# A gate table stored in reading order, with the expert gathers spread over the table's building

## The chip, the cores and the metric

The kernel runs on one NeuronCore of a Trainium2 chip. The metric is the device time of one execution in microseconds (us), the median of several runs. Engines are named as the profile names them: PE (TensorE matmuls; PEld are its weight loads), DVE (VectorE), ACT (ScalarE), POOL (GpSimd, which also issues the gathers) and SP (SyncE, which issues most loads).

## The reference, cut to what matters

One decoder block over 256 tokens of width 2048 in fp32. The first sub-layer (sparse attention and a pooling mixer) is not touched. The second is the PEER retrieval: 8 heads pick 16 of 16384 single-neuron experts for each token.

```python
q = jnp.einsum('bsd,de->bse', h, w_peer_q).reshape(B, S, PEER_HEADS, 2, PEER_QDIM // 2)
sub = jnp.einsum('bshpd,hpnd->bshpn', q, peer_keys, ...)
s_top, i_top = lax.top_k(sub, PEER_TOPK)
cand = s_top[..., 0, :, None] + s_top[..., 1, None, :]
...
best, pos = lax.top_k(cand, PEER_TOPK)
experts = jnp.take_along_axis(cand_idx, pos, axis=-1)
gates = jax.nn.softmax(best, axis=-1)
...
a = jax.nn.gelu(jnp.einsum('cd,ced->ce', hc, peer_u[ec]), approximate=False)
out = jnp.einsum('ce,ced->cd', a * gc, peer_v[ec])
```

## The kernel before, in words

The kernel computes 224 of the 256 tokens densely: all 16384 experts' activations, multiplied by a gate table that is zero where an expert was not picked. The other 32 tokens (AS) are done sparsely: their experts' rows are gathered from memory and reduced on DVE. Both share the last two thirds of the time, which is a loop of 512 steps of the same size on PE. A step takes half of an expert block's table: 8 weight blocks of 128x128, each with a product with 448 columns (L934: the rounded weights `wH` with both halves of the activations) and one with 224 (L935: the remainder `wL`). Steps 0 to 255 are the up stage (table `in_u`), 256 to 383 the first down half and 384 to 511 the second (table `in_v`).

The program's order is written out by hand, engine by engine. In step k, `ahead(k)` issues a table load on SP (into one of 4 `raw` buffers) and splits the half of step k+2: a cast on ACT (`wH`, L125) and a subtraction on DVE (`wL`, L126). Then come the products, and then `spend(rate)`, which adds the rate to a credit and takes pieces of DVE work off a list of tasks until the credit is used up. A piece names its DVE time in us (0.69 for one operation of the gate building, 2.37 for a sparse reduction); a piece that names none (`yield None`) ends the step's turn. Each engine works through its own queue in order, so a piece that waits holds up all that stands behind it.

The list is, in this order: `routing(0)` (the experts of the first 128 tokens), the gate table of tokens 32 to 127, `routing(1)`, the gate table of the rest, `tokens_h`, two loads of `in_ada` left over from the first sub-layer, then 32 `sparse_up` and 32 `sparse_down`. A `sparse_up(n)` reduces the gathered rows `r` (L814, "r<-r,hs"; two buffers) and lets POOL issue the gather for n+2 (L809). `gates_build(x)` makes the gates of 8 tokens: four DVE operations on fp16 (L750, L757), 16 small matmuls (L771), and two copies on ACT (L781) into a staging tile `hs`, of which POOL writes every second one's 1 MB to `gdram` (L783). The staging tile has one buffer: its next ACT copy waits until the write has landed.

Near the end of the up stage and through the first down half, `gate_table(b)` reads 8 expert blocks' gates on SP (L906, `gb`, one buffer, so it waits for both multiplications with the last one), `gate_load` reads 4 blocks of activations `ab` from `adram` (L902), `gate_mul` multiplies them on DVE (L918), and POOL writes them back to `adram` (L923) for the second half, except for 9 of 32 groups (`kept`), which stay in the space of `hHL`. `gate_split` (L928, L929) makes the two halves that the down products take.

Of the kernel before, what the change touches and what calls it, by code (L numbers as in the profile page):

```python
# [9 lines left out]
F32 = mybir.dt.float32  # L10
F32R = mybir.dt.float32r
# [8 lines left out]
P = 128  # L20
T = 256
D = 2048
ND = 16
# [4 lines left out]
SH1, SC1, GT1, SH2, SC2, GT2 = (16 * i for i in range(6))  # L28
AS = 32
N = T - AS  # L30
# [1 line left out]
KGROUPS = ((0, 4), (4, 10), (10, 16))  # L32
NGU = 43
RAW = 4
R_K, R_Y, R_GA, R_WO, R_PQ = 0.6, 0.75, 0.7, 0.6, 0.3
TB = 8
R_UP, R_D1, R_D2 = 0.97, 0.3, 0.75
KEPT = 9
GATE_SCALE = 2.0 ** 15


# [1 line left out]
def kernel(  # L43
# [23 lines left out]
    nc = tc.nc  # L67
# [8 lines left out]
    cb = const.tile([P, D], F32, name="cb")  # L76
# [69 lines left out]
    def add_bias(i, n):  # L146
        dve.tensor_tensor(mod[:, i:i + n], modr[:, i:i + n], bada[:, i:i + n], ALU.add)
# [29 lines left out]
    bg = []  # L177
# [544 lines left out]

    def routing(t):
        for h in range(8):
            if t:
                yield from top_list(t, h)
            yield from top_cand(t, h)
        yield from decode(t, 0)
        yield from decode(t, 1)
        yield from gates_of(t)  # L730

    gdram = dram.tile([P, N // 16, P, 16], F32, name="gdram")
    adram = dram.tile([P, P, N], F32, name="adram")
    made = {}

# [38 lines left out]

    def gates_out(x):
        if x % 2 == 0:
            made["stage"] = px.tile([P, D], F32, name="hs")
        stage = made["stage"].rearrange("p (i t) -> p i t", t=16)
        for y in range(2):
            t0 = 8 * (x % 2) + 4 * y  # L780
            act.mul(stage[:, :, t0:t0 + 4], made["g", y].rearrange("p (t i) -> p i t", i=P), 1.0 / GATE_SCALE)  # L781
        if x % 2 == 1:
            nc.gpsimd.dma_start(out=gdram[:, (x - AS // TB) // 2].rearrange("p i t -> p (i t)"), in_=made["stage"])  # L783
            made["gates"] = x

    def tokens_h(q):
# [48 lines left out]
            fetch(n + 2, vrows)  # L835
        yield 2.36

    def ada_later(i):
        raw = load(ada_in[i])
        yield None  # L840
        yield None
        ada_sum(raw, i)
        yield 2.37

    def tasks_up():
        yield from routing(0)
        for x in range(AS // TB, P // TB):
            yield from gates_build(x)
        yield from routing(1)
        for x in range(P // TB, T // TB + 1):  # L850
            yield from gates_build(x)
        for q in range(4):
            yield from tokens_h(q)
        fetch(0, urows)
        fetch(1, urows)
        yield None
        for n in range(AS):
            if bg:
                yield from ada_later(bg.pop(0))
            elif "gt2" not in made:  # L860
                add_bias(GT2, 16)
                made["gt2"] = True
            yield from sparse_up(n)
        for n in range(AS):
            yield from sparse_down(n)

    work = tasks_up()
    credit[0] = 0.0

    def spend(budget):  # L870
        credit[0] = min(credit[0] + budget, 4.0)
        while credit[0] > 0.0:
            cost = next(work, "end")
            if cost is None or cost == "end":
                return cost
            credit[0] -= cost

    raws = {}

# [11 lines left out]
    def half(k):  # L891
        return split(raws[k // 2][:, 1024 * (k % 2):1024 * (k % 2) + 1024])

    def kept(h):
        return h % 3 == 0 and 0 < h <= 3 * KEPT

    def gate_load(n):
        h = n % (P // 4)
# [4 lines left out]

    def gate_table(b):
        made["gb", b] = px.tile([P, N // 16, 8, 16], F32, name="gb")
        nc.sync.dma_start(out=made["gb", b], in_=gdram[:, :, 8 * b:8 * b + 8])  # L906

    def gate_mul(h):
        if kept(h):
            if "keep" not in made:  # L910
                made["keep"] = main.tile([P, ND, 2, T], F32R, name="hHL").rearrange("p a b t -> p (a b t)")
            o = 4 * N * (h // 3 - 1)
            dst = made["keep"][:, o:o + 4 * N].bitcast(F32).rearrange("p (i n) -> p i n", n=N)
            made["ab", P // 4 + h] = dst
        else:
            dst = made["ab", h]
        i = 4 * (h % 2)
        dve.tensor_tensor(dst.rearrange("p i (g t) -> p i g t", t=16),  # L918
                          made["ab", h].rearrange("p i (g t) -> p i g t", t=16),
                          made["gb", h // 2][:, :, i:i + 4].rearrange("p g i t -> p i g t"), ALU.mult)  # L920
        made["ab", h] = dst
        if not kept(h):
            nc.gpsimd.dma_start(out=adram[:, 4 * h:4 * h + 4], in_=dst)  # L923
# [8 lines left out]
    def mm2(ps, w, off, xHL, start, stop):  # L932
        wH, wL = w[0][:, off:off + P], w[1][:, off:off + P]
        pe.matmul(ps[:, :2 * N].rearrange("p (a n) -> p a n", a=2), wH, xHL, start=start, stop=False)  # L934
        pe.matmul(ps[:, :N], wL, xHL[:, 0], start=False, stop=stop)  # L935

    engines = {mybir.EngineType.PE, mybir.EngineType.DVE, mybir.EngineType.Activation, mybir.EngineType.Pool,
               mybir.EngineType.SP}
# [30 lines left out]
    for k in range(2 * P):  # L969
        e, f = k // 2, k % 2  # L970
        ahead(k)
        if f == 0:
            ps = accp.tile([P, 512], F32, name="acc")
        w = ws.pop(k)
        for d in range(8):
            mm2(ps, w, d * P, hHL[:, 8 * f + d, :, AS:], f == 0 and d == 0, f == 1 and d == 7)
        if f == 1:
            pend.append(lambda e=e, ps=ps: up_add(e, ps))
        spend(R_UP)
        if k == 2 * P - 24:  # L980
            assert made["gates"] == T // TB - 1
            gate_table(0)
            for h in range(3):
                gate_load(h)
        if k in (2 * P - 8, 2 * P - 7):
            gate_mul(k - 2 * P + 8)
        if k == 2 * P - 6:
            gate_table(1)
        if k == 2 * P - 5:
            gate_split(0)  # L990
        if k == 2 * P - 4:
            gate_load(3)
# [22 lines left out]
        nc.sync.dma_start(out=out[:, 0:8, :], in_=xT[:, 0:8, :])  # L1015

    for hf in range(2):
        assert hf == 0 or made["gt2"]
        po = [accp.tile([P, 512], F32, name="acc") if q < 6 else gps.tile([P, 512], F32, name="gp") for q in range(8)]

        def products(e, w, j):
            mm2(po[j], w, P * j, made["act", 32 * hf + e // 4][:, e % 4], e == 0, e == P - 1)

        for e in range(P):
            k = 2 * P + P * hf + e
            h = e // 4
            if e < P - 1:
                ahead(k)
            if e < P - 2:
                w = ws.pop(k)  # L1030
# [12 lines left out]
            if hf == 0 and e % 8 == 5 and b + 2 < P // 8:  # L1043
                gate_table(b + 2)
            if e % 4 == 1 and n + 1 < 2 * (P // 4):
                gate_split(n + 1)
            if e % 4 == 2 and n + 4 < 2 * (P // 4):
                gate_load(n + 4)
            done = spend(R_D2 if hf else R_D1)
            if hf and done == "end" and "sum" not in made:  # L1050
                made["sum"] = True
                pend.append(lambda: sparse_sum(po))
                pend.append(lambda: pend.append(lambda: sparse_out(po)))
# [80 lines left out]
```

## Time and profile before

| What | us |
|---|---|
| median of 3 runs (lowest, highest) | 2155.93 (2154.45, 2156.39) |
| the profiled execution | 2165.35 |
| its span, first to last instruction | 2163.6 |
| PE busy | 2080.1 (96%) |
| DVE busy | 1704.4 (79%) |
| ACT busy | 1039.6 (48%) |
| POOL busy | 142.5 (7%) |

The profiled execution is 9.4 us longer than the median of the runs. PE is busy nearly everywhere, so time is found where it stands idle or where its weight blocks come more slowly. The up stage begins at 793.6 us of the span, the first down half at about 1486, the second at about 1825.

### The profile page before, as it was taken

Reading aid. Unit: us, or ns where it says so; the run is one execution under the profiler, and the core shown is the slowest. Engines: PE = TensorE matmul, PEld = TensorE weight load, DVE = VectorE, ACT = ScalarE, POOL = GpSimd, SP = SyncE. Lnnn points to the kernel's source line nnn. Section 1 sums busy time; section 2 is a strip of 40 time slices with the busy share of each in tenths; the row PEclk is TensorE's granted clock in tenths of the full one; section 3 lists DMA queues with packets and bytes.
Section 4 is the critical chain, followed back from the end, with each engine's and each line's share of the span. In section 5 each row is a group of like instructions: output and inputs, shape, how many; then the busy total and the mean of one; then the engine's idle time right before and its main releaser. Section 6 shows DMA issues by size and latency. Waiting matters only on the chain.

```text
span 2163.6 us, 35340 instructions
## 1 busy us (share of the span) xinstructions
PE 2080.1 (96%) x14192; PEld 1965.9 (91%) x14192; DVE 1704.4 (79%) x2424; ACT 1039.6 (48%) x1405; POOL 142.5 (7%) x120
## 2 busy tenths in 40 slices
PE   6999999999898999999999999989999999999998
PEld 4998997899898999999999999888999998999998
DVE  7888888767877778778887775877777678888855
ACT  4543342463334445555555555444544455544544
POOL 0000000000000000000000000221111012222100
PEclk8999999999899999999999999998999999999999
DMA  9887886768875656676666777999999999999964
GB/s 348 326 314 294 303 307 247 278 242 304 311 291 200 219 212 228 235 262 249 231 231 248 255 279 269 363 399 342 371 361 373 370 374 346 374 375 375 365 221 143
DMA packets 142933, 640.29 MB, mean 296 GB/s; under 512 B 11449, under 2 KB 42193, under 8 KB 94257
## 3 DMA queue, kind: packets, MB, share of 16 engines
q1 hardware_dynamic: 124690, 530.82, 67.5%
q0 software_dynamic: 13472, 92.55, 11.4%
q10 hardware_dynamic: 4608, 14.68, 1.7%
q8 instruction: 111, 1.82, 0.3%
q14 instruction: 52, 0.43, 0.1%
HBM read 595.95 MB, written 42.02 MB: 295 GB/s over the span
## 4 chain that ended last, share of the span: by engine, by line
PE 47%; issue 24%; DMA 13%; DVE 10%; ACT 3%; POOL 1%; SPq 0%; DVEq 0%; ACTq 0%; POOLq 0%
PE acc L934 16%; PE acc L935 8%; DMA raw<-in_ada_dram 6%; PE acc L137 5%; DMA raw<-in_v_dram 5%; PE acc L135 5%; PE acc L136 5%; PE gp L934 4%; DVE raw L140 4%; DVE wL L126 3%; PE gp L935 2%; ACT wH L125 2%; DMA raw<-in_u_dram 1%; PE acc L510 1%; DMA r<-in_urow_dram,idxS 0%
## 5 line engine op out<-in xcount | busy, mean ns | idle before, releaser
L125 ACT CAST wH<-raw 128x1024 fp32r<-128x1024 f32 (+2 forms) x738 | 751.1, 1022 | 926.3 <-PE acc L934 278.5
L126 DVE TENSOR_TENSOR wL<-raw,wH 128x1024 fp32r<-128x1024 f32 (+2 forms) x738 | 871.3, 1188 | 329.1 <-ACT wH L125 326.4
L934 PE MATMUL acc<-hHL,wH 128*128 128x448 f32 x2048 | 655.7, 377 | 0.5 <-ACT r L601 0.5
L935 PE MATMUL acc<-hHL,wL 128*128 128x224 f32 x2048 | 546.8, 267 | 9.3 <-DVE wL L126 9.2
L934 PE MATMUL acc<-aHL,wH 128*128 128x448 f32 x1536 | 503.6, 378 | 7.6 <-DVE ast L961 5.0
L935 PE MATMUL acc<-aHL,wL 128*128 128x224 f32 x1536 | 409.6, 267 | 6.5 <-DVE wL L126 6.2
L934 PEld LDWEIGHTS acc<-hHL,wH 128*128 128x128 f32 x2048 | 386.3, 189 | 29.2 <-ACT r L601 0.7
L935 PEld LDWEIGHTS acc<-hHL,wL 128*128 128x128 f32 x2048 | 393.3, 192 | 12.2 <-DVE wL L126 12.1
L135 PE MATMUL acc<-hHL,wH 128*128 128x256 f32 x1200 | 345.9, 289 | 19.2 <-ACT wH L125 17.9
L137 PE MATMUL acc<-hHL,wL 128*128 128x256 f32 x1200 | 342.0, 287 | 8.7 <-DVE wL L126 8.6
L136 PE MATMUL acc<-hHL,wH 128*128 128x256 f32 x1200 | 342.1, 286 | 0.1
L934 PEld LDWEIGHTS acc<-aHL,wH 128*128 128x128 f32 x1536 | 290.8, 189 | 29.8 <-DVE ast L961 5.3
L935 PEld LDWEIGHTS acc<-aHL,wL 128*128 128x128 f32 x1536 | 296.2, 193 | 12.2 <-DVE wL L126 12.1
L135 PEld LDWEIGHTS acc<-hHL,wH 128*128 128x128 f32 x1200 | 232.4, 194 | 23.9 <-ACT wH L125 21.4
L140 DVE CUSTOM_DVE_ANT_0 raw<-raw,cb 128x2048 f32<-128x2048 f32 x96 | 219.7, 2288 | 43.4 <-DMA raw<-in_ada_dram 37.6
L137 PEld LDWEIGHTS acc<-hHL,wL 128*128 128x128 f32 x1200 | 231.5, 194 | 11.8 <-DVE wL L126 11.5
L136 PEld LDWEIGHTS acc<-hHL,wH 128*128 128x128 f32 x1200 | 232.5, 194 | 0.8 <-DVE hHL L574 0.3
L934 PE MATMUL gp<-aHL,wH 128*128 128x448 f32 x512 | 177.1, 377 | 0.4 <-DVE xT L998 0.4
L935 PE MATMUL gp<-aHL,wL 128*128 128x224 f32 x512 | 135.4, 264 | 0.0
L934 PEld LDWEIGHTS gp<-aHL,wH 128*128 128x128 f32 x512 | 96.4, 188 | 8.0 <-DVE xT L998 1.0
L935 PEld LDWEIGHTS gp<-aHL,wL 128*128 128x128 f32 x512 | 98.2, 192 | 0.0
L814 DVE CUSTOM_DVE_ANT_0 r<-r,hs 128x2048 f32<-128x2048 f32 x32 | 73.2, 2287 | 15.1 <-DMA r<-in_urow_dram,idxS 15.1
(250 smaller groups left out, 2070.5 us busy)
## 6 DMA issues: line engine op xcount, KB each, us to landing
raw<-in_u_dram SPq DMA_DIRECT2D x128, 1024.0 KB, 5.1
raw<-in_v_dram SPq DMA_DIRECT2D x128, 1024.0 KB, 9.5
raw<-in_ada_dram SPq DMA_DIRECT2D x96, 1024.0 KB, 5.7
raw<-in_wgrp_dram SPq DMA_DIRECT2D x43, 768.0 KB, 6.0
ab<-adram SPq DMA_DIRECT2D x55, 448.0 KB, 8.8
raw<-in_ybr_dram SPq DMA_DIRECT2D x16, 1024.0 KB, 6.6
raw<-in_wga_dram SPq DMA_DIRECT2D x16, 1024.0 KB, 4.8
raw<-in_wout_dram SPq DMA_DIRECT2D x16, 1024.0 KB, 5.0
```

Source lines behind the costliest of these rows:

```text
L125: act.copy(wH[:, :n], src)
L126: dve.tensor_tensor(wL[:, :n], src, wH[:, :n], ALU.subtract)
L135: pe.matmul(ps, wH, xH, start=start, stop=False, **kw)
L136: pe.matmul(ps, wH, xL, start=False, stop=False, **kw)
L137: pe.matmul(ps, wL, xH, start=False, stop=stop, **kw)
L140: dve.tensor_tensor_reduce(raw, raw, cb, scale=1.0, scalar=0.0, op0=ALU.mult, op1=ALU.add, accum_out=modr[:, i:i + 1])
L510: pe.matmul(ps, ybr[0][:, o:o + P], pooled[k], start=k == 0, stop=k == 7)
L814: dve.tensor_tensor_reduce(rows, rows, made["h"], scale=1.0, scalar=0.0, op0=ALU.mult, op1=ALU.add, accum_out=aS[:, n:n + 1])
L934: pe.matmul(ps[:, :2 * N].rearrange("p (a n) -> p a n", a=2), wH, xHL, start=start, stop=False)
L935: pe.matmul(ps[:, :N], wL, xHL[:, 0], start=False, stop=stop)
```

## The change

The gate table lies in `gdram` in the order in which `gate_table` reads it: a read takes 7168 contiguous bytes per partition instead of 14 pieces of 512 bytes, and a write now makes 16 pieces of 512 bytes per partition instead of one of 8192. The staging tile is `cb` instead of `hs`; `hs` holds the sparse tokens' activations from early on. The task list becomes two streams, `gates` and `sparse`. `tokens_h` and the first two gathers come before the gate building. `spend` takes a sparse piece ahead of a gate piece whenever the sparse work so far, times 3.2, lies at least 70 us under the gate work so far. The up stage's rate is 1.0 while the gate stream lives and 0.5 after it (before: 0.97); the first down half's is 0.2 (before: 0.3). The two late loads of `in_ada` move into the projection ahead of the up stage (rate 0.45 instead of 0.3). 13 groups stay on the chip instead of 9, and the first gate table is read 14 steps ahead of the end of the up stage instead of 24.

```diff
-R_K, R_Y, R_GA, R_WO, R_PQ = 0.6, 0.75, 0.7, 0.6, 0.3
+R_K, R_Y, R_GA, R_WO, R_PQ = 0.6, 0.75, 0.7, 0.6, 0.45
-R_UP, R_D1, R_D2 = 0.97, 0.3, 0.75
-KEPT = 9
+R_UP, R_D1, R_D2 = 1.0, 0.2, 0.75
+R_SU, G_LEAD = 3.2, 70.0
+KEPT = 13
...
-    gdram = dram.tile([P, N // 16, P, 16], F32, name="gdram")
+    gdram = dram.tile([P, P // 8, N // 16, 8, 16], F32, name="gdram")
...
         if x % 2 == 0:
-            made["stage"] = px.tile([P, D], F32, name="hs")
+            made["stage"] = const.tile([P, D], F32, name="cb")
...
-            nc.gpsimd.dma_start(out=gdram[:, (x - AS // TB) // 2].rearrange("p i t -> p (i t)"), in_=made["stage"])
+            nc.gpsimd.dma_start(out=gdram[:, :, (x - AS // TB) // 2],
+                                in_=made["stage"].rearrange("p (b i t) -> p b i t", i=8, t=16))
...
+    def tasks_first():
+        yield from routing(0)
+        for h in range(8):
+            yield from top_list(1, h)
         for q in range(4):
             yield from tokens_h(q)
         fetch(0, urows)
         fetch(1, urows)
+        yield from tasks_gates()
...
     def spend(budget):
         credit[0] = min(credit[0] + budget, 4.0)
+        held = set()
         while credit[0] > 0.0:
-            cost = next(work, "end")
-            if cost is None or cost == "end":
-                return cost
-            credit[0] -= cost
+            ready = [n for n in streams if n not in held]
+            if "gat" not in made and "sparse" in ready:
+                ready.remove("sparse")
+            if "gates" in streams and "sparse" in ready and spent["sparse"] * R_SU > spent["gates"] - G_LEAD:
+                ready.remove("sparse")
+            if "sparse" in ready and "gates" in ready:
+                ready.remove("gates")
+            if not ready:
+                return
+            n = ready[0]
+            cost = next(streams[n], "end")
+            if cost == "end":
+                del streams[n]
+            elif cost is None:
+                held.add(n)
+            else:
+                credit[0] -= cost
+                spent[n] += cost
...
     def kept(h):
-        return h % 3 == 0 and 0 < h <= 3 * KEPT
+        return h % 2 == 1 and 3 <= h < 3 + 2 * KEPT
...
-        nc.sync.dma_start(out=made["gb", b], in_=gdram[:, :, 8 * b:8 * b + 8])
+        nc.sync.dma_start(out=made["gb", b], in_=gdram[:, b])
...
-        spend(R_UP)
-        if k == 2 * P - 24:
+        spend(R_UP if "gates" in streams else 0.5)
+        if k == 2 * P - 14:
```

What POOL issues during the gate building, before: the 14 writes of the gate table (`gdram<-hs`), and only then the gathers of the sparse tokens (`r<-in_urow_dram`).

```order
L783 DMA gdram<-hs 128x2048 x14
L809 DMA r_14327<-in_urow_dram,idxS 128x2048 x18
L923 DMA adram<-ab 128x896
```

The same place in the changed kernel: the writes, now of 2048 pieces each (`gdram<-cb`), and the gathers alternate.

```order
L809 DMA r_10409<-in_urow_dram,idxS 128x2048 x3
L782 DMA gdram<-cb 2048x1x128 x2
L809 DMA r_10409<-in_urow_dram,idxS 128x2048
L782 DMA gdram<-cb 2048x1x128
...
L782 DMA gdram<-cb 2048x1x128
L809 DMA r_10409<-in_urow_dram,idxS 128x2048 x6
L948 DMA adram<-ab 128x896 x2
```

So the sparse stream starts with the gate building and no longer after it: up to the first write of gated activations POOL has issued 23 gathers instead of 18.

What DVE does near step 212 of the up stage, before: a sparse reduction (`ISA r,aS<-r,hs`) every second or third step, one at a time, between the splits (`wL`) and the sums of the up stage (`ast`).

```order
L126 TENSOR_TENSOR wL<-raw,wH 128x1024 x2
L961 TENSOR_TENSOR ast<-acc,join 128x224
L814 ISA r_14327,aS<-r_14327,hs 128x2048
L814 ISA aS 128x1
L126 TENSOR_TENSOR wL<-raw,wH 128x1024 x2
L961 TENSOR_TENSOR ast<-acc,join 128x224
L814 ISA r_14327,aS<-r_14327,hs 128x2048
```

And in the changed kernel at steps 224 to 231, where the gate stream ends: a reduction in step 224, two in step 229 and one in step 231.

```order
L756 TENSOR_TENSOR o_14692<-o_14692,gT_8327 128x1024
L814 ISA r_10409,aS<-r_10409,hs 128x2048
L814 ISA aS 128x1
L127 TENSOR_TENSOR wL<-raw,wH 128x1024 x2
...
L127 TENSOR_TENSOR wL<-raw,wH 128x1024
L814 ISA r_10409,aS<-r_10409,hs 128x2048
L814 ISA aS 128x1
L814 ISA r_10409,aS<-r_10409,hs 128x2048
L814 ISA aS 128x1
L127 TENSOR_TENSOR wL<-raw,wH 128x1024
L990 TENSOR_TENSOR ast<-acc,join 128x224
L127 TENSOR_TENSOR wL<-raw,wH 128x1024
L814 ISA r_10409,aS<-r_10409,hs 128x2048
```

After that the reductions stand five steps apart up to step 246 and four to five apart to the end of the up stage.

## Rows read from the trace of the kernel before

**Rows 1.** The page: span.
```profile
span 2163.6 us, 35340 instructions
```

**Rows 2.** Windows, L934 alone (a matmul per weight block): us, busy (count), clock, DMA.
```profile
1350.00:1486.00 136.00, 125.49 (x385) 74.36 (x386) 0.96 0.96 366
1486.00:1534.00 48.00, 42.88 (x131) 25.44 (x130) 0.93 0.96 357
1534.00:1824.00 290.00, 280.44 (x892) 167.09 (x891) 1.00 1.01 367
1900.00:2000.00 100.00, 100.00 (x320) 59.91 (x320) 1.00 0.98 375
```

**Rows 3.** Waits between 1350 and 1500 us: total, times, longest.
```profile
DVE r L814 <- DMA r<-in_urow_dram,idxS: 15.1, 9, 3.6
```

**Rows 4.** Timeline of POOL, DVE and PE around 1457 us: start, us, what.
```profile
1446.28 1.67 POOL L809 DMA_INDIRECT r<-in_urow_dram,idxS  x1 [6.31 <-DVE aS L814]
1457.28 2.29 DVE L814 CUSTOM_DVE_ANT_0 r<-r,hs 128x2048 f32<-128x2048 f32 x1 [3.63 <-DMA r<-in_urow_dram,idxS]
1459.49 2.36 DVE L126 TENSOR_TENSOR wL<-raw,wH 128x1024 fp32r<-128x1024 f32 x2
1460.77 0.56 PE L935 MATMUL acc<-hHL,wL 128*128 128x224 f32 x1 [3.22 <-DVE wL L126]
```

**Rows 5.** Window just after that wait, all engines: PE count, then PEclk.
```profile
1460.80:1466.40 5.60, 5.60 (x19) 5.21 (x20) 4.73 (x6) 1.12 (x2) 1.36 (x2) 0.50 0.81 306
```

**Rows 6.** Timeline of SP at one read of the gate table.
```profile
1591.05 0.54 SPq L906 DMA_DIRECT2D gb<-gdram  x1
1591.67 4.52 SPq L887 DMA_DIRECT2D raw<-in_v_dram  x1
```

**Rows 7.** Waits between 1534 and 1744 us.
```profile
ACT wH L125 <- DMA raw<-in_v_dram: 50.3, 18, 4.4
PE acc L935 <- DVE wL L126: 4.8, 12, 0.8
```

**Rows 8.** Loads of `in_v`, from issue to landing: first half (1534:1744), then second (1840:2000).
```profile
DMA to landing us min/median/max: 9.3/11.5/14.1
...
DMA to landing us min/median/max: 5.1/7.3/9.4
```

**Rows 9.** Windows, all engines: projection ahead of the up stage; second down half.
```profile
712.00:786.00 74.00, 74.00 (x623) 74.00 (x623) 56.37 (x129) 31.27 (x48) 0.00 (x0) 1.00 0.62 227
1840.00:2020.00 180.00, 180.00 (x1151) 172.19 (x1150) 154.71 (x113) 90.87 (x90) 38.57 (x23) 1.00 0.97 374
```

**Rows 10.** Groups on POOL: busy us, mean ns of one.
```profile
L809 POOL DMA_INDIRECT r<-in_urow_dram,idxS x32 | 52.7, 1646 | 235.1 <-DVE aS L814 232.9 <-DMA adram<-ast 1.6 <-issue 0.6
L783 POOL DMA_DIRECT2D gdram<-hs x14 | 7.5, 535 | 407.8 <-ACT hs L781 407.8
L712 POOL DMA_DIRECT2D gS<-cand x4 | 2.0, 497 | 8.1 <-DVE cand L708 8.1
```

**Rows 11.** DMA issues: KB each, median us to landing.
```profile
gdram<-hs POOLq DMA_DIRECT2D x14, 1024.0 KB, 4.4
gb<-gdram SPq DMA_DIRECT2D x16, 896.0 KB, 9.6
r<-in_urow_dram,idxS POOLq DMA_INDIRECT x32, 9.5
```

**Rows 12.** Timeline of ACT, POOL and DVE around two writes of the gate table.
```profile
925.36 0.58 POOL L783 DMA_DIRECT2D gdram<-hs  x1 [25.09 <-ACT hs L781]
930.94 1.08 ACT L781 ACTIVATE hs<-gp 128x512 f32<-128x512 f32 x2
958.19 1.41 DVE L757 TENSOR_TENSOR o<-o,gT 128x1024 f16<-128x1024 f16 x2
958.24 0.53 POOL L783 DMA_DIRECT2D gdram<-hs  x1 [16.58 <-ACT hs L781]
1315.05 0.53 POOL L783 DMA_DIRECT2D gdram<-hs  x1 [17.94 <-ACT hs L781]
```

More of the change, by code (lines that the diff above doesn't have):

```diff
@@ L724, in routing @@
         for h in range(8):
-            if t:
-                yield from top_list(t, h)
             yield from top_cand(t, h)
@@ L836, in sparse_down, with tasks_gates @@
         yield 2.36
[L838 to L846, printed above, removed]
+    def tasks_gates():
         for x in range(AS // TB, P // TB):
@@ L851, in tasks_up, with tasks_sparse @@
             yield from gates_build(x)
+        made["all"] = True
+    def tasks_sparse():
+        for n in range(AS):
+            yield from sparse_up(n)
+        for n in range(AS):
+            yield from sparse_down(n)
+    def tasks_first():
+        yield from routing(0)
+        for h in range(8):
+            yield from top_list(1, h)
         for q in range(4):
@@ L855, in tasks_up @@
         fetch(1, urows)
[L856 to L868, printed above, removed]
+        yield from tasks_gates()
+    streams = {"gates": tasks_first(), "sparse": tasks_sparse()}
+    spent = {"gates": 0.0, "sparse": 0.0}
     def spend(budget):
         credit[0] = min(credit[0] + budget, 4.0)
+        held = set()
         while credit[0] > 0.0:
-            cost = next(work, "end")
-            if cost is None or cost == "end":
-                return cost
-            credit[0] -= cost
+            ready = [n for n in streams if n not in held]
[16 more added lines that the diff above has]
+                spent[n] += cost
+    credit[0] = 0.0
     raws = {}
@@ L892, in half, with home @@
         return split(raws[k // 2][:, 1024 * (k % 2):1024 * (k % 2) + 1024])
+    homes = {}
     def kept(h):
-        return h % 3 == 0 and 0 < h <= 3 * KEPT
+        return h % 2 == 1 and 3 <= h < 3 + 2 * KEPT
+    def home(h):
+        q = (h - 3) // 2
+        if q < 9:
+            if "hHL" not in homes:
+                homes["hHL"] = main.tile([P, ND, 2, T], F32R, name="hHL").rearrange("p a b t -> p (a b t)").bitcast(F32)
+            flat = homes["hHL"][:, 4 * N * q:4 * N * q + 4 * N]
+        elif q < 11:
+            if "cb" not in homes:
+                homes["cb"] = const.tile([P, D], F32, name="cb")
+            flat = homes["cb"][:, 4 * N * (q - 9):4 * N * (q - 9) + 4 * N]
+        else:
+            return px.tile([P, 4, N], F32, name="ast", bufs=2)
+        return flat.rearrange("p (i n) -> p i n", n=N)
     def gate_load(n):
@@ L905, in gate_table @@
         made["gb", b] = px.tile([P, N // 16, 8, 16], F32, name="gb")
-        nc.sync.dma_start(out=made["gb", b], in_=gdram[:, :, 8 * b:8 * b + 8])
+        nc.sync.dma_start(out=made["gb", b], in_=gdram[:, b])
     def gate_mul(h):
         if kept(h):
[L910 to L913, printed above, removed]
+            dst = home(h)
             made["ab", P // 4 + h] = dst
@@ L935, in mm2 @@
         pe.matmul(ps[:, :N], wL, xHL[:, 0], start=False, stop=stop)
+    while bg:
+        pace(1.0)
+    add_bias(GT2, 16)
     engines = {mybir.EngineType.PE, mybir.EngineType.DVE, mybir.EngineType.Activation, mybir.EngineType.Pool,
@@ L1017 @@
     for hf in range(2):
-        assert hf == 0 or made["gt2"]
         po = [accp.tile([P, 512], F32, name="acc") if q < 6 else gps.tile([P, 512], F32, name="gp") for q in range(8)]
@@ L1048 @@
                 gate_load(n + 4)
-            done = spend(R_D2 if hf else R_D1)
-            if hf and done == "end" and "sum" not in made:
+            spend(R_D2 if hf else R_D1)
+            if hf and not streams and "sum" not in made:
                 made["sum"] = True
```

## The prediction, made before the run

> **What bounds the kernel now.** I read the page first. The span is 2163.6 us [rows 1] and PE is busy nearly all of it, so shares say little. The next view is therefore the windows, for the L934 matmuls alone: there is one for each weight block, so their count is a clock of progress. Where nothing disturbs PE, in the second down half, 320 blocks take 100 us, 0.3125 us each, 2.5 us for a step of eight [rows 2]. Time above count times 0.3125 is lost time. It lies in three places [rows 2]:
>
> - the tail of the up stage, 1350 to 1486 us: 136 - 385 x 0.3125 = 15.7 us
> - the change to the down stage, 1486 to 1534: 48 - 131 x 0.3125 = 7.1 us
> - the first down half, 1534 to 1824: 290 - 892 x 0.3125 = 11.2 us
>
> Together 34.0 us, 1.6% of the span. The earlier part of the up stage also falls below this pace, but there PE works on the gate building's small matmuls, which stay. So the change can win some 34 us and no more, and each place needs its cause.
>
> In the tail the waits name it: DVE's sparse reduction waits for its gather, nine times, 15.1 us in all, 3.6 at the longest [rows 3]. The timeline shows one such wait through to its end [rows 4]. POOL issues a gather at 1446.28, the reduction of these rows starts 11.0 us later, after 3.63 us of waiting, the split `wL` that stands behind it on DVE is late by that, and PE idles for 3.22 us. So DVE's lead over PE is worth only 3.63 - 3.22 = 0.4 us at such a spot. After the idle time the granted clock is 0.50, the lower of the two levels (1.2 GHz): in 5.6 us there are 19 matmuls, 9.5 blocks, worth 3.0 us at the full clock [rows 5]. The wait costs its idle time and 2.6 us on top.
>
> In the first down half ACT waits for the loads of `in_v` (50.3 us in 18 waits, 4.4 at the longest), and PE for the splits behind them [rows 7]. SP shows why [rows 6]: after a read of the gate table the next load's issue occupies SP for 4.52 us. The read has 128 x 14 pieces. These loads land in 11.5 us in the first half and in 7.3 in the second, where no gate table is read [rows 8]; and there PE has no lost time at the same 367 to 375 GB/s [rows 2, 9]. So the gate table's reads do the harm, not the bytes.
>
> **The change, part by part.**
>
> *Order of the table.* 16 reads shrink from 1792 pieces to 128. SP still issues each only after the second multiplication with the table before (one buffer `gb`), but the load behind it no longer takes 4.5 us to issue, and lands nearer to 7.3 than 11.5 us after that. Both are larger than the 4.4 us that ACT waits at the longest [rows 6 to 8], so nearly all of that wait goes. From the first half's 11.2 us I take 9 and leave 2 for steps in which a reduction and multiplications stand together on DVE. The two bounds are 0 left (as in the second half) and 9 left (rival 2).
>
> *The change to the down stage.* It has the same pattern: a gate table read and a load of `in_v` behind it, with late reductions on DVE. 2 us stay, because the first products need a PSUM buffer that the last sum of the up stage still holds. 5 are gained.
>
> *Streams and rates.* 23 gathers instead of 18 leave POOL ahead of the first write of gated activations, most of them beside the gate building, eight steps or more apart, that is 20 us or more, against 9.5 us from issue to landing [rows 11]. None of these should wait. After the gate stream the rate is 0.5, so a reduction of 2.37 us comes every 4.7 steps, 11.9 us; with two buffers a gather has over 20 us. That removes the 15.7 us of the tail, but for one place, which the order of the instructions shows: two reductions in step 229 and a third in step 231. The third one's gather can only be issued after the first of the two. It takes 9.5 to 11.0 us [rows 4, 11], say 10.4. Meanwhile DVE has the second reduction (2.3 us) and two splits (2.4 us) [rows 4] with a short sum between them, 5.1 us with 0.4 for the sum. It then waits for 10.4 - 5.1 = 5.3 us, PE idles for 5.3 - 0.4 = 4.9, and the clock falls, 2.6 more [rows 5]. New cost: 7.5 us, with bounds of 3.7 (a gather of 9.5 us, half of the clock's part) and 9.
>
> The other bursts (three list pieces in step 41 instead of two in step 78; a reduction beside two gate pieces in step 224) I take at 2 us.
>
> *Two loads of `in_ada` moved.* Each is a DVE operation over 2048 columns like the sparse reduction, of 2.3 us [rows 4]. In the projection DVE is busy for 56.37 of 74 us and PE for all 74 [rows 9]: two more fit, at no cost. Without that cover they'd cost 4.6 us.
>
> *13 groups kept.* Four writes of 448 KB less in the first half, four reads less in the second. The second half has nothing to gain (180.00 of 180 us busy [rows 9]). In the first half it eases the same loads; I count nothing extra.
>
> *The writes.* The price is paid here: 14 writes now have 2048 pieces each. No row shows such a write. POOL's time for one: 0.497 us with 32 pieces, 0.535 with 128 [rows 10]; at that slope 2048 pieces take 1.3 us, at a price in full proportion to pieces (0.535 / 128) 8.6 us, by the gather's 1.646 us for 128 rows 26 us. From issue to landing it takes 4.4 us now; the gate table's reads in 512-byte pieces take 9.6 for seven eighths of the bytes, in busier surroundings [rows 11]. Who waits: ACT's next copy into the staging tile, and behind it the casts. It comes 930.94 - 925.36 = 5.6 us after the issue [rows 12]; nine of the 13 gaps keep these three steps, the others have five or more. ACT's lead is larger than DVE's: it waited up to 4.4 us for a load while PE never idled for more than 0.8 [rows 7], a lead of some 3.5 us. So PE pays from a landing of about 9 us on. I take 2 us on POOL and a landing of 7: no cost. The row with 32 and 128 pieces is nearest, since it is the same kind of instruction; the others are kept for rival 1.
>
> **A rule of the Trainium skill** bears on this. The writes lie beside DVE's fp16 operations, as they do now: the write at 958.24 ran inside an operation of DVE (958.19 to 959.60) and took 0.53 us, like the one at 1315.05 after the gate building [rows 12]. The Trainium skill (SBUF — State Buffer, "SBUF: two separate sides") says that while DVE runs an operation in a two-port mode, GpSimd can't write DMA descriptors and the transfer starves. This trace doesn't show that here, at 128 pieces. By that rule a list of 2048 could be held up by the 1.4 us pairs that fill each step, and I would give rival 1 a chance of 0.2 instead of 0.13.
>
> **The sum.** 34.0 us lost now; after: 7.5 + 2 (bursts) + 2 (change of stage) + 2 (first half) = 13.5. Gain 20.5 us: a span of 2143. The profiled execution took 2165.35 us, the runs' median is 2155.93; the 9.4 us between them stay, so 2155.9 - 20.5 = 2135.4, say **2136 us**.
>
> **Rivals.**
>
> 1. *Slower: the writes of 2048 pieces hold up ACT.* Against it: the slope between 32 and 128 pieces. For it: no row with more. With POOL at 8.6 us a write lands at about 4.4 + 8.1 + 1 = 13.5, PE idles for 4.5 us in nine gaps, and each such idle time brings 0 to 2.6 us of lower clock: 40 to 64 us, so net 20 to 44 slower, 2175 to 2200. It cancels the gain where a landing takes 9 + 20.5 / 9 = 11.3 us. Chance 0.13.
> 2. *The first half stays as it is,* because SP still stops at each gate table read until the second multiplication is done, and the `in_v` loads queue up behind. For it: the stop is unchanged. Against it: rows 6. 9 of the 11.2 us stay and 4 in the change of stage, 9 more than forecast: 2144 us. Chance 0.15.
> 3. *The burst at steps 229 to 231 is covered* (an earlier landing, or a lead of DVE that the gates' slower steps built up): 7.5 us more gained, 2128 us. Against it: DVE is busy for nearly the whole step there. Chance 0.14.
> 4. *It cancels out:* writes land at some 11 us, or the bursts in the gate building cost 1 us each in twenty steps. 2152 to 2160. Chance 0.05.
>
> The forecast (2130 to 2143) has 0.53. Faster by over 0.2% (4.3 us, about what a measurement of this kernel can tell from no change): 0.53 + 0.15 + 0.14 = 0.82, less 0.02 for a mix of rivals 2 and 4, so 0.80. Within 0.2%: 0.06. Slower: 0.14. The range reaches down to the forecast with everything gained but 2 us (2155.9 - 32 = 2124) and up to no change (2157): it leaves out rival 1 and little else.
>
> **What would show each step right or wrong.** In the changed kernel's windows the blocks after the gate building should come at 0.3125 us, but for one idle time of some 5 us and a clock of 0.50 near step 234. The waits of DVE for gathers should fall from 15.1 us to some 6 in one wait. The issue after a gate table read should take SP about 0.4 us, the `in_v` loads should land in 8 us or less in the first half, and ACT's 50.3 us of waits for them should go. POOL's `gdram` writes should last under 3 us and land in under 9, and ACT should not wait for them. The forecast is wrong if ACT's copies into `cb` wait for the write before (rival 1), if the first half's lost time stays above 6 us (rival 2), or if no idle time stands at step 234 (rival 3).

## The result, and the profile after

| | before | changed |
|---|---|---|
| median of 6 runs each, us (lowest, highest) | 2155.2 (2150.8, 2158.3) | 2181.7 (2177.0, 2188.3) |
| ratio, 95% interval | | 1.0105 (1.0084 to 1.0126) |
| profiled execution / its span, us | 2165.35 / 2163.6 | 2180.97 / 2179.2 |

The changed kernel is 26.5 us slower. The forecast was 2136 us, the range 2124 to 2157: wrong in sign. The ratio is not the quotient of the two medians (1.0123), which lies within its interval; by the interval the loss is 18 to 27 us. In the profiled executions the difference is 15.6 us, since that of before lay 10.2 us above the median of the table.

Windows of the changed kernel, L959 alone (the line that was L934; columns as in [rows 2]): the two parts of the gate building, the end of the up stage, the first down half with the change of stage, the second down half.

```profile
950.00:1150.00 200.00, 170.77 (x521) 99.70 (x521) 0.96 0.70 249
1228.00:1440.00 212.00, 184.73 (x557) 107.23 (x557) 0.96 0.74 264
1440.00:1517.00 77.00, 70.28 (x216) 41.84 (x215) 0.93 0.91 353
1517.00:1807.00 290.00, 287.92 (x920) 172.26 (x919) 1.00 0.94 364
1900.00:2000.00 100.00, 100.00 (x320) 59.82 (x319) 1.00 0.96 361
```

The last three rows are near the forecast. The end of the up stage loses 77 - 216 x 0.3125 = 9.5 us, against 15.7 in [rows 2]; the first down half with the change of stage loses 290 - 920 x 0.3125 = 2.5, against 11.2 and 7.1 there. The loss is in the first two rows: there the mean granted clock is 0.96. Before, the same two parts looked like this:

```profile
926.00:1100.00 174.00, 166.14 (x523) 97.87 (x523) 1.00 0.70 247
1160.00:1340.00 180.00, 164.22 (x510) 95.28 (x509) 1.00 0.75 271
```

521 blocks take 200 us now, 523 took 174; 557 take 212, 510 took 180, so 557 would have taken 180 + 47 x 0.3125 = 194.7. Less some 2 us for gate matmuls of which the first window has more, these parts take about 24 + 17 = 41 us longer. The whole up stage, from its first product to the first down product, takes 728.4 us instead of 692.4. The waits of the changed kernel between 950 and 1520 us name the cause:

```profile
ACT cb L780 <- DMA gdram<-cb: 53.3, 8, 10.5
PE gp L770 <- ACT cb L780: 20.7, 5, 6.5
DVE r L814 <- DMA r<-in_urow_dram,idxS: 6.9, 2, 6.4
PE acc L959 <- ACT wH L126: 5.8, 1, 5.8
```

ACT waits for the landing of the write before, up to 10.5 us, before it may copy into `cb` again; in six places (five and one) PE then idles for 26.5 us in all. Each of the six stands behind a write that had a gather issued ahead of it on POOL, 1.1 to 3.1 us ahead in five and 9.1 us in one. One of them in the timeline (start, us, what):

```profile
1011.70 1.15 POOL L809 DMA_INDIRECT r<-in_urow_dram,idxS  x1 [57.79 <-DVE aS L814]
1012.84 1.26 POOL L782 DMA_DIRECT2D gdram<-cb  x1
1013.09 0.69 DVE L749 TENSOR_TENSOR o<-iota,idxT 128x1024 f16<-128x1024 f16 x1
1013.20 0.33 SPq L119 DMA_DIRECT2D raw<-in_u_dram  x1
...
1026.57 1.09 ACT L780 ACTIVATE cb<-gp 128x512 f32<-128x512 f32 x2 [10.38 <-DMA gdram<-cb]
1027.21 1.01 PE L770 MATMUL gp<-o,o 128*128 128x128 f16 x8 [6.47 <-ACT cb L780]
...
1028.62 1.22 DVE L127 TENSOR_TENSOR wL<-raw,wH 128x1024 fp32r<-128x1024 f32 x1 [9.84 <-ACT wH L126]
```

POOL issues a gather, 1.1 us later the write, and SP a table load 0.4 us after that: three transfers of 1 MB within 1.5 us. The write lands 13.6 us after its issue; ACT was ready for its copy 3.4 us after it. Behind ACT's copy stand PE's gate matmuls and the casts, and behind these DVE. The clock then is 0.50, the lower of the two levels (1.2 GHz), with 17 matmuls in 3.5 us:

```profile
1027.50:1031.00 3.50, 3.50 (x17) 3.28 (x16) 2.38 (x4) 2.28 (x4) 0.00 (x0) 0.50 0.00 0
```

POOL itself is not what is slow. The group of the writes (busy us, mean ns of one), then the time from issue to landing, for the 11 of the 14 whose landing the trace has:

```profile
L782 POOL DMA_DIRECT2D gdram<-cb x14 | 16.2, 1160 | 142.5 <-ACT cb L780 141.7 <-ACT wH L126 0.8
```
```profile
DMA to landing us min/median/max: 6.7/9.9/14.6
```

A list of 2048 pieces takes POOL 1.16 us; 1.3 was the forecast by the slope. The shortest landing is 6.7; 7 was taken for all. What differs is the company. DMA traffic of the changed kernel while two writes were under way, the one at 1012.84 (13.6 us) and the one at 1036.23 (6.8 us); q0 is POOL's queue, q1 SP's, q10 ACT's:

```profile
DMA packets 705, 4.21 MB, mean 309 GB/s; under 512 B 64, under 2 KB 64, under 8 KB 320
...
q0 software_dynamic: 416, 2.10, 43.2%
q1 hardware_dynamic: 288, 2.10, 40.5%
```
```profile
q0 software_dynamic: 272, 1.05, 60.8%
q10 hardware_dynamic: 133, 0.42, 15.1%
q1 hardware_dynamic: 60, 0.41, 15.0%
```

The slow one shares its time with a whole gather and two table loads, 4.21 MB in all. The quick one has its queue to itself, and beside it 0.41 MB of a load and 0.42 MB of a write of activations, 1.90 MB in all.

The forecast burst, for [rows 4]: one idle time of 6 us near step 234, behind a reduction that waits for its gather.

```profile
1443.52 1.01 POOL L809 DMA_INDIRECT r<-in_urow_dram,idxS  x1 [1.32 <-DVE aS L814]
...
1454.99 2.29 DVE L814 CUSTOM_DVE_ANT_0 r<-r,hs 128x2048 f32<-128x2048 f32 x1 [6.39 <-DMA r<-in_urow_dram,idxS]
1458.48 0.56 PE L960 MATMUL acc<-hHL,wL 128*128 128x224 f32 x1 [5.99 <-DVE wL L127]
```

And for [rows 6 to 8] SP at a read of the gate table, the one wait for `in_v` that is left between 1510 and 1730 us (50.3 us before), and the landing of these loads:

```profile
1592.34 0.34 SPq L934 DMA_DIRECT2D gb<-gdram  x1
1592.78 0.43 SPq L899 DMA_DIRECT2D raw<-in_v_dram  x1
```
```profile
ACT wH L126 <- DMA raw<-in_v_dram: 2.4, 1, 2.4
```
```profile
DMA to landing us min/median/max: 7.5/8.2/9.9
```

### The profile page after: what moved, and what is told of

Its sections match the earlier page's. It is cut to its first block, busy times and chain, and to the rows that moved or that the text cites. A ratio compares the mean times of both kernels' runs of the same rounds, so it can differ in the third digit from the quotient of the medians.

```text
span 2179.2 us, 35303 instructions
## 1 busy us (share of the span) xinstructions
PE 2082.4 (96%) x14192; PEld 1972.6 (91%) x14192; DVE 1706.8 (78%) x2424; ACT 1041.3 (48%) x1405; POOL 141.8 (7%) x116
## 3 DMA queue, kind: packets, MB, share of 16 engines
q0 software_dynamic: 14944, 90.71, 11.2%
## 4 chain that ended last, share of the span: by engine, by line
PE 62%; issue 19%; DVE 9%; DMA 5%; ACT 2%; POOL 2%; POOLq 0%; DVEq 0%; ACTq 0%
PE acc L959 23%; PE acc L960 11%; PE acc L138 6%; PE acc L136 6%; PE acc L137 6%; PE gp L959 5%; DMA raw<-in_ada_dram 4%; DVE raw L141 3%; PE gp L960 2%; DVE wL L127 2%; ACT wH L126 1%; POOL r L809 1%; POOL gdram L782 1%; PE acc L511 1%; DMA raw<-in_wgrp_dram 1%
## 5 line engine op out<-in xcount | busy, mean ns | idle before, releaser
L959 PE MATMUL acc<-hHL,wH 128*128 128x448 f32 x2048 | 663.6, 380 | 6.2 <-ACT wH L126 5.8
L960 PE MATMUL acc<-hHL,wL 128*128 128x224 f32 x2048 | 549.3, 268 | 8.1 <-DVE wL L127 8.0
L959 PE MATMUL acc<-aHL,wH 128*128 128x448 f32 x1536 | 500.0, 376 | 4.4 <-DVE join L1041 2.4
L959 PEld LDWEIGHTS acc<-hHL,wH 128*128 128x128 f32 x2048 | 390.6, 191 | 36.5 <-ACT wH L126 6.0
L960 PE MATMUL acc<-aHL,wL 128*128 128x224 f32 x1536 | 407.2, 265 | 0.8 <-DVE wL L127 0.8
L960 PEld LDWEIGHTS acc<-hHL,wL 128*128 128x128 f32 x2048 | 396.9, 194 | 9.9 <-DVE wL L127 9.9
L959 PEld LDWEIGHTS acc<-aHL,wH 128*128 128x128 f32 x1536 | 289.3, 188 | 27.5 <-issue 2.8
L960 PEld LDWEIGHTS acc<-aHL,wL 128*128 128x128 f32 x1536 | 294.3, 192 | 1.1 <-DVE wL L127 1.1
L959 PE MATMUL gp<-aHL,wH 128*128 128x448 f32 x512 | 177.3, 376 | 0.4 <-DVE xT L1027 0.4
L960 PE MATMUL gp<-aHL,wL 128*128 128x224 f32 x512 | 135.7, 265 | 0.0
L959 PEld LDWEIGHTS gp<-aHL,wH 128*128 128x128 f32 x512 | 96.7, 189 | 8.6 <-DVE xT L1027 1.0
L960 PEld LDWEIGHTS gp<-aHL,wL 128*128 128x128 f32 x512 | 98.4, 192 | 0.0
L809 POOL DMA_INDIRECT r<-in_urow_dram,idxS x32 | 52.7, 1646 | 521.2 <-DVE aS L814 461.4
```

Source lines behind the costliest of these rows:

```text
L809: nc.gpsimd.indirect_dma_start(out=made["gat"][:, n % 2], out_offset=None, in_=table, in_offset=bass.IndirectOffsetOnAxis(ap=idxS[:, n:n + ...
```

## The experiments

The kernel before was timed again beside every batch of runs. Its medians there are 2159.4 us (runs 1 to 4), 2160.1 (5 to 8), 2163.5 (9) and 2161.2 (10 and 11), against 2155.2 in the table above. A ratio is to the kernel before of the same batch; a difference of medians from two batches is uncertain by some 4 to 8 us, so the length of the up stage in the profiled executions stands beside it where it matters.

The theories before the first four runs. A: a write issued shortly behind a gather lands late, and with one staging tile ACT and PE wait for it. B: the small pieces are slow by themselves among the table loads. C: DVE has too much to do at rate 1.0.

**1. Two staging tiles.** The changed kernel, where every second staging tile is in the space of `gb`, free until the tables are read:

```diff
-            made["stage"] = const.tile([P, D], F32, name="cb")
+            made["stage"] = const.tile([P, D], F32, name="cb") if x % 4 == 0 else px.tile([P, D], F32, name="gb")
...
```

> The changed kernel with a second staging buffer for the gate table's writes (the space of the later gate table tile), so that ACT's copies wait for the write before the last. Theory A (a write that POOL issues shortly after a gather lands late, the single staging tile keeps ACT waiting, and PE behind it): the six waits of 2 to 6.5 us go, some 44 us, and the burst near step 234 stays: 2137 us, within 8. Rival B (small pieces are slow among the table's loads): the same, since the buffer hides any landing under 17 us. Rival C (the waits are a sign of DVE being overbooked at rate 1.0 with reductions among the gate pieces): no change, 2175 to 2185 us.

Measured: 2136.3 us, ratio to before 0.9872 (0.9839 to 0.9905), by the medians 45 us less than the changed kernel. The up stage falls from 728.4 to 686.7 us, by 41.7. The writes land as late as in the changed kernel (6.8 to 15.5 us in the ten landings that the trace has), no copy waits for them, and one large idle time is left, the burst:

```profile
1415.54 0.56 PE L960 MATMUL acc<-hHL,wL 128*128 128x224 f32 x1 [7.36 <-DVE wL L127]
```

So the wait for the staging tile is the whole of the loss. C falls: DVE does the same work at the same rate.

**2. The writes on ACT's queue,** otherwise the changed kernel:

```diff
-            nc.gpsimd.dma_start(out=gdram[:, :, (x - AS // TB) // 2],
+            act.dma_start(out=gdram[:, :, (x - AS // TB) // 2],
```

> The changed kernel with the 14 writes of the gate table issued by ACT instead of POOL, so that they don't stand in the gathers' queue; one staging tile. Theory A: every write lands in 5 to 7.5 us, no wait for the staging tile, 2137 us, within 8, if ACT loses nothing by issuing. Rival B: landings of 10 to 14 us remain in part of the writes, and the waits with them: over 2165 us. Rival C: 2175 to 2185 us.

Measured: 2165.0 us, ratio 1.0014 (0.9993 to 1.0036). A miss for A: the place behind the gather in POOL's queue is not all of it. The waits stay, shorter in sum (37.6 us instead of 53.3); the two landings that the trace has are 15.3 and 17.5 us:

```profile
ACT cb L780 <- DMA gdram<-cb: 37.6, 5, 9.9
```

**3. Only the new order of the table,** in the kernel before; the gathers come after the gate building:

```diff
-    gdram = dram.tile([P, N // 16, P, 16], F32, name="gdram")
+    gdram = dram.tile([P, P // 8, N // 16, 8, 16], F32, name="gdram")
...
-        nc.sync.dma_start(out=made["gb", b], in_=gdram[:, :, 8 * b:8 * b + 8])
+        nc.sync.dma_start(out=made["gb", b], in_=gdram[:, b])
```

> The kernel before with the new order of the gate table alone (writes of 2048 pieces, reads of 128), all gathers after the gate building as before. Theory A: no gather stands ahead of a write, so writes land in 6.5 to 7.5 us, ACT doesn't wait; the first down half loses nearly nothing (before: 11 us) and the change of stage less: 2140 us, within 4. Rival B: part of the writes land in 10 us or more, and the gain of the reads is eaten: 2150 to 2180 us.

Measured: 2142.8 us, ratio 0.9902 (0.987 to 0.9933). 14 writes of 2048 pieces, all quick: the trace has seven of the landings, and behind every one of the 14 ACT's next copy starts within 7.0 us of the issue.

```profile
DMA to landing us min/median/max: 6.6/6.7/6.9
```

B in its plain form falls: small pieces among the table loads that run in this part are not slow.

**4. The old order of the table in the changed kernel:** the edits of run 3 the other way.

> The changed kernel with the old order of the gate table (writes of 128 pieces of 8 KB, reads of 1792), gathers among the gate building as in the change. Theory A: writes just behind a gather still land in 9 to 12 us, the waits for the staging tile shrink to some 20 us, and 5 to 8 us of the first half's loss come back: 2158 to 2170 us. Rival B: all writes land in 4.3 to 5 us as before the change, no waits: 2140 to 2150 us.

Measured: 2164.2 us, ratio 1.0016 (0.9996 to 1.0037). With 8 KB pieces the writes land in 4.6 us at best and 12.9 at worst (eight landings):

```profile
ACT cb L780 <- DMA gdram<-cb: 42.3, 7, 10.5
```
```profile
DMA to landing us min/median/max: 4.6/7.4/12.9
```

Large pieces don't cure it; of the up stage's 41.7 us, some 19 (728.4 - 709.2) come with the small ones, which land 2 us later at best. Runs 3 and 4 also tell what healed the first down half, in L935 of the one and L958 of the other over 1534 to 1824 us: lost are 2.5 and 1.3 us, against 11.2.

```profile
1534.00:1824.00 290.00, 288.25 (x920) 172.36 (x919) 1.00 0.97 377
```
```profile
1534.00:1824.00 290.00, 289.61 (x924) 173.26 (x923) 1.00 0.97 357
```

**5. Each gather behind the next write.** The changed kernel, with one staging tile; a gather is put off and issued just after the next write of gates:

```diff
             made["gates"] = x
+            while late:
+                fetch(*late.pop(0))
...
+    late = []
...
-        if n + 2 < AS:
-            fetch(n + 2, urows)
-        else:
-            fetch(n + 2 - AS, vrows)
+        while late:
+            fetch(*late.pop(0))
+        late.append((n + 2, urows) if n + 2 < AS else (n + 2 - AS, vrows))
+        if "all" in made:
+            fetch(*late.pop(0))
...
```

> The changed kernel, but while gates are built a gather is issued just behind the next write of gates (POOL) and no longer right after its reduction, so that no gather stands ahead of a write; one staging tile, as in the change. Theory A, after the miss of the run with the writes on ScalarE's queue: a write is late because it starts only when the gather ahead of it on POOL's queue is through, and then runs beside the next table load. Then every write lands in 6.5 to 8 us, no wait of ScalarE for cb is left while gates are built, and the time falls by the some 44 us which those waits cost, to 2137 (2132 to 2143). Rival D: it is the sharing of the transfer engines between gathers and writes, whichever is issued first. Then the write that has a gather behind it still lands in 10 us or more, waits stay, and the time is 2160 or more.

Measured: 2145.1 us, ratio 0.9919 (0.9886 to 0.9951), by the medians 37 us less than the changed kernel. Between the two expectations: eight of the writes land in 6.6 to 7.4 us, six in 9.4 to 12.9, one idle time of 4.0 us is left in the gate building, and the burst costs more than in the changed kernel (10.8 us idle). A gather behind the write does little: six of the eight quick writes have one issued 1.4 to 3.1 us behind them. Four of the six late ones have a table load issued within 0.3 us of them; the other two, of 9.7 and 12.9 us, have not.

```profile
ACT cb L780 <- DMA gdram<-cb: 16.3, 5, 7.9
PE gp L770 <- ACT cb L780: 4.8, 2, 4.0
```

**6 to 8. Without the burst.** The saved-up credit is cut where a stream ends; in run 6 alone, in run 7 with two staging tiles, in run 8 with the gathers behind the writes:

```diff
                 del streams[n]
+                credit[0] = min(credit[0], 0.5)
```

> The changed kernel, but the saved-up credit is cut to 0.5 where a stream of work ends, so that the two reductions at steps 229 and 231 don't come in a burst; one staging tile, as in the change. Theory: the burst costs the 9 us that VectorE lacks near step 234, and nothing else of the 44 us changes: 2172 (2168 to 2176). Rival: VectorE is behind at the end of the up stage whatever the burst, the loss only moves: 2181.

> Two staging tiles (as in the first run) and the credit cut to 0.5 where a stream ends. Theory: both losses go, the 44 us and the burst: the 2136 of two staging tiles less 9 gives 2127 (2123 to 2131). Rival: as with the burst alone, the loss only moves: 2136.

> One staging tile, gathers issued behind the next write of gates, and the credit cut to 0.5 where a stream ends. Theory A: as two staging tiles with the cut, 2128 (2123 to 2134), without more space. Rival D: waits of some 40 us stay, 2165 or more.

Measured: 2170.2 us, ratio 1.0045 (1.0022 to 1.0069); 2127.2 us, ratio 0.9843 (0.9817 to 0.987); 2130.0 us, ratio 0.9852 (0.982 to 0.9884). All three by the theory. In run 7 the end of the up stage has no stall over 1.0 us left (L960, 136 - 418 x 0.3125 = 5.4 us beside 15.7 before, and the gate building's last matmuls are in it):

```profile
1350.00:1486.00 136.00, 131.79 (x418) 78.16 (x417) 1.00 0.92 351
```

Run 7 beats both kernels: 33 us under before in its batch.

Run 6 builds its gates as the changed kernel does, and its trace has all 14 landings:

```profile
DMA to landing us min/median/max: 6.7/11.2/15.2
```

They fall into groups. Five writes with a gather issued 1.1 to 4.4 us ahead of them land in 13.2 to 15.2 us (four of them have a load within 1.3 us as well; the one that has not takes 14.4), two with one 9.1 and 9.5 us ahead in 11.5 and 12.6, two with no gather near but a table load issued within 0.3 us in 9.6 and 10.9, the other five in 6.7 to 8.1.

**9. The kernel of run 3, writes on ACT's queue.** It asks why run 2 missed.

> The kernel before with the new order of the table alone, and the gate table's writes issued by ScalarE; no gather runs while gates are built. It says why the changed kernel with ScalarE's writes missed. Theory A, as mended by that run: there the write no longer stood behind the gather, but the two shared the transfer engines, and the gather took most of them. Without gathers such writes land in 8 us or less, no wait for the staging tile is left, and the time is that of POOL's writes in this kernel, 2143 (2138 to 2149). Rival E: on ScalarE's queue 2048 pieces are slow beside any load. Then the landings are 10 us or more here too, ScalarE waits for the staging tile, and the time is 2155 or more.

Measured: 2145.2 us, ratio 0.9912 (0.9891 to 0.9934). The three landings that the trace has are 5.7 to 5.8 us, and behind every write ACT's next copy starts within 7.2 us of the issue. So it is not the queue alone. But it leaves open whether a load can do what a gather does, because in runs 3 and 9 the two don't meet: the writes come every six steps and the loads every two, and in run 3 the next load is issued 1.8 us or more behind a write, the last one 2.5 us or more ahead of it.

**10 and 11. The gate building one step later,** in the kernels of runs 3 and 9, which moves all writes to the other step of a load:

```diff
         yield from routing(0)
+        yield None
         for x in range(AS // TB, P // TB):
```

> The kernel before with the new order of the table, and the whole gate building one step later, so that a write is issued at the other one of the two steps of a table load: some 2.7 us later, and so about when the next load of in_u is issued and no longer some 3 us ahead of it. No gather runs while gates are built. It tells apart two readings of the late landings. Reading F: any transfer of 1 MB issued shortly ahead of the write delays it, a table load as well as a gather, and the gathers do their harm also by moving loads into the write's way. Then these writes land in 9 to 11 us, and the time is 2143 to 2150, since PE pays little below 9 us plus its lead. Reading G: only a gather delays a write. Then they land in 6.6 to 6.9 us as without the shift, and the time stays at 2143 (2138 to 2149).

> As the run with the gate building one step later, but with the writes issued by ScalarE, for the miss of the changed kernel with ScalarE's writes. Reading F: a load issued with the write delays it on this queue too, to 9 us or more, so that this miss was due to loads as well as gathers. Reading G: 5.7 to 6.1 us as in the unshifted kernel. Time 2145 to 2155 by F, 2145 by G.

Measured in run 10: a load is now issued between 0.2 us ahead of each write and 1.0 behind it, and the writes land in 9.5 to 11.5 us (nine landings), in run 11 in 9.0 to 14.2 (six), without any gather.

```profile
DMA to landing us min/median/max: 9.5/10.7/11.5
```

DMA traffic beside one write, in run 3 (973.39 to 980.1 us) and in run 10 (941.65 to 952.38):

```profile
q0 software_dynamic: 272, 1.05, 60.3%
q1 hardware_dynamic: 102, 0.70, 25.2%
```
```profile
q1 hardware_dynamic: 253, 1.94, 55.6%
q0 software_dynamic: 272, 1.05, 24.6%
q10 hardware_dynamic: 144, 0.46, 11.1%
```

Reading F is shown: loads alone delay a write. Beside it move 0.7 MB of a load in run 3, nearly two whole loads and a write of activations in run 10. This accounts for run 2 in part. Of the five writes there that ACT waits for, three have a gather issued 0.8 to 9.0 us ahead of them (waits of 9.0 to 9.9 us) and one a load 1.1 us ahead (4.2 us); the fifth (4.8 us), with loads some 3 us off on either side, stays unexplained. ACT's queue also moves the 1 MB in 2064 packets where POOL's takes 272; whether that matters among other transfers, no run separates. The times missed: 2158.4 us, ratio 0.9976 (0.9942 to 1.0011), and 2160.5, ratio 1.0001 (0.998 to 1.0022), where up to 2150 and 2155 were expected. In run 10 it is not ACT's wait for the staging tile in the gate building that costs PE: 34.3 us in 13 waits, none over 4.1, and PE idles 0.3 us behind them.

```profile
ACT hs L781 <- DMA gdram<-hs: 34.3, 13, 4.1
...
PE gp L771 <- ACT hs L781: 0.3, 1, 0.3
```

Of the 13.1 us between the two profiled spans (2146.9 and 2160.0) 9 arise in scattered places ahead of the down stage; which of them go back to the landings stays open.

## Why the prediction was wrong

**The step that failed** is "I take 2 us on POOL and a landing of 7: no cost". Both numbers hold for a write with no gather ahead of it and the table loads some 2 to 5 us off: 1.16 us on POOL, 6.7 to landing. What was overlooked is what the change does to the company of a write. It puts a gather of 1 MB ahead of it, on the same queue, and it moves the writes against the table loads. Before, the last load was issued 3.2 us or more ahead of each of the 14 writes and the next 1.9 to 3.0 us behind it; in the changed kernel eight of the 14 have a load within 1.6 us. That the 2.3 us reductions among the splits shift them is the likely reason, but no run separates it. The landings of run 6 show both effects side by side, runs 3 and 10 the second by itself (6.7 to 10.7 us by one step), run 5 the first in part. The late writes of the changed kernel that had no gather near them made PE idle nowhere; all six idle times go with gathers. The prediction costed the gathers' own wait ("None of these should wait") and not that of those who wait behind them. It should have looked at what is in flight beside a write: 4.21 MB moved in the 13.6 us of the one, 3.45 MB in the 10.7 of run 10, 1.75 MB in the 6.7 of run 3. (These are bytes counted in the write's own time, so they describe the delay and don't yet predict it.)

**The price was rival 1's, the mechanism half.** Its chain (ACT waits for the staging tile, PE idles, the clock falls) is the one that came, and its 2175 to 2200 holds 2181.7. Its cause, 8.6 us on POOL, is not there, so that the price fits is partly luck. It had PE idle for 4.5 us in nine gaps; there were six, 4.4 us each, 26.5 in sum. Of the 41.7 us by which run 1 shortens the up stage some 15 are left; the mean clock of 0.96 over the 412 us of the first two windows makes up to 16 us of that. The bound "PE pays from a landing of about 9 us on" took ACT's copy to come 5.6 us behind the issue. In five of the six places it was ready after 3.4 to 5.9 us, and PE idled for what ACT waited beyond 3.9 us (4.7 in one). In run 10 it was ready only after 6.6 to 8.9 us between two writes, and a median landing of 10.7 us leaves PE 0.3 us idle behind the copies.

**The steps that held.** The losses that should remain were 13.5 us: 7.5 for the burst, 2 for other bursts, 2 for the change of stage, 2 in the first half. They are 9.5 (the window 1440 to 1517), 1.3 (an idle time at 900.6) and 2.5 for the last two together, 13.3 in sum. Run 1, which removes the waits alone, gains 5.7 us in the up stage (692.4 to 686.7) and 14.4 in the first down half with the change of stage (339.2 to 324.8); the sum had 6.2 and 14.3. That its median of 2136.3 us meets the forecast of 2136 is in part luck, since the kernel before was at 2159.4 in that batch. The burst has the place and the cause that were given; it was mis-sized by 2 us, since the gather took 11.5 us from its issue to the reduction (10.4 were assumed) and DVE waited for 6.4, not 5.3. The lower bound given for it, 3.7, doesn't follow from its own terms (a gather of 9.5 us with half of the clock's part makes 9.5 - 5.1 - 0.4 + 1.3 = 5.3); the upper one, 9, names no terms, and the 9.5 us lie above it. Run 6 shortens the up stage by 8.5 us without the burst, run 7 by 9.2 against run 1.

**The first down half was right in sum and too narrow in cause.** The gate table's reads were to do the harm, "not the bytes". Run 3 agrees in part: the loads still land in 11.7 us (median), yet the second load behind a gate table read is issued 2.6 us after the read (1583.17 to 1585.73) and no longer 6.2 (1591.05 to 1597.22), and ACT's waits for `in_v` fall from 50.3 to 14.4 us. But run 4 keeps the reads of 1792 pieces and loses only 1.3 us, with loads that land in 9.7. So the rest of the change does it too; fewer writes and reads of activations and fewer reductions are the likely cause, not separated here. From the first down product to that of the second half it takes 339.2 us before, 327.8 in run 3, 325.4 in run 4 and 323.1 in the changed kernel: either half of the change gives most of it.

**The two loads of `in_ada`** cost nothing that shows: the up stage begins at 788.0 us of the span, 5.6 earlier than before. In the eight profiles with the new projection it begins at 782.0 to 788.6, in the five with the old one at 786.1 to 795.2. The sum has no term for that, and why it is earlier stays open.

**The rule on the shared port.** Eleven writes of 2048 pieces ran beside DVE's fp16 operations in 1.12 to 1.26 us (the one at 1012.84 beside the operation at 1013.09), three away from them in 1.14 to 1.18. So this trace again doesn't show what the Trainium skill (SBUF — State Buffer, "SBUF: two separate sides") describes, a GpSimd that can't write descriptors meanwhile. Whether these operations, which read two tensors, use such a mode at all, no run here shows.

A rule that would have helped stands in the Trainium skill (DMA: Bandwidth & Descriptors, "Issuing engines are not separate DMA queues"): transfers issued by different engines end up on the same 16 DMA engines and interleave. Runs 2 and 11 agree: on ACT's own queue a write still landed in 9.0 to 17.5 us with others about (eight landings), in 5.7 to 5.8 in run 9, with the loads some 3 us off (three).

## What to carry to other kernels

A transfer's time to landing belongs to the place, not to the instruction: before taking it from the old trace, list what the new order issues in the microseconds ahead of it and with it, on all queues, and add the megabytes. Here a gather 1 to 4 us ahead cost some 6 to 8 us of landing, one 1.4 to 3.1 us behind on the same queue nearly none. Ask of each single buffer that a transfer empties how long its next writer can wait, and who stands behind that writer; here a second staging tile in space that was free turned a loss of 26.5 us into a gain of 23, and with the burst removed of 33. Where transfers recur in a fixed ratio of steps, one step can decide whether they meet.

## What the runs showed of the hardware

- A list of 2048 pieces of 512 bytes takes POOL 1.11 to 1.26 us, one of 128 pieces 0.53 to 0.60; with no gather ahead and the loads some 2 to 5 us off, the 1 MB lands in 6.6 to 6.9 us instead of 4.3 to 5.4.
- The same pieces issued by ACT land in 5.7 to 5.8 us there (run 9), and with other transfers closer by in up to 17.5 us (run 2).
- A table load issued with the write, and the next some 5 us behind it, instead of 3 us off on either side, make 10.7 us of 6.7 (runs 3 and 10). A gather issued 1.1 to 4.4 us ahead, in four of five cases with a load within 1.3 us as well, makes 13.2 to 15.2 (run 6). A gather issued 1.4 to 3.1 us behind leaves 6.6 to 7.0 (run 5).
- After 6.5 us without a matmul the granted clock was 0.50 in the 3.5 us that follow; before the change it was so after 3.2 us [rows 5].
